# The sample's attention in blocks of 16 rows by 8 columns, with queries and keys put in column order

## The chip, the cores and the metric

The kernel runs on one core of a Trainium2 chip. The metric is the device time of one execution in microseconds; the time shown is the median of three. Five engines run side by side, each through its own list of instructions in a fixed order: PE (matmuls and transposes), DVE (vector), ACT (scalar), POOL (GpSimd) and SP, which here only issues DMAs. They wait for each other through semaphores.

## What is computed

One encoder layer is applied to two sequences, a sample of 1024 tokens and a prompt of 512 tokens, both with 1024 channels. Tokens form a grid of 64 columns, so the sample has 16 rows and the prompt 8. Cut to what matters:

```python
proj = rms_norm(x, norm_g) @ w_in        # u_pool, g_pool, q, k, v, g_attn, 512 columns each
pool_out = pool_mixer(u_pool) * silu(g_pool)
q = rms_norm(q per head) * 64 ** -0.5;  k = rms_norm(k per head)      # 8 heads of 64
# a query in row r, column c sees 8 rows from clip(r - 4, 0, rows - 8)
# and 16 columns from clip(c - 8, 0, 48), with a learned bias by row and column offset
p = softmax(q . k + rpb[h, row offset, column offset])
y = x + concat(pool_out, (p @ v) * silu(g_attn)) @ w_out
```

Products are made in split precision: a value is kept as a rounded high part and a low part (high plus low is the value), and a product is two or three matmuls.

## The kernel before

**Order of the work.** The code records every instruction in a planner (class `Plan`), which gives each a cost and a priority, follows what each tile is read and written by, and then issues all instructions in the order of its own timeline. So all instructions of the profile bear one line, L330, and one has to go by tile names. Where code says `plan.choice()`, the planner also decides the engine. Matmuls of the projections have a lower priority (`MAIN`); PE's list has those of the attention between them where the planner had them ready.

**Stages.** The sample is first. For each of four pairs of heads p: `project_qkv` multiplies the tokens, 128 a tile (t = 0 to 7), into PSUM banks `acc_s_t`; ACT copies them to `qkv_s` (a ring of four); q and k are normalised on DVE, and two transposes per token tile put them into a PSUM bank `ptq_s`, channels by tokens, for two token tiles together (t0 = 0, 2, 4, 6). From there ACT writes the high parts of q and k (`q`, `k`) and DVE the low parts, which sum with the high parts to the values. v goes to DRAM (`vd`) and back into `vs`. Gates (`accg`), the pooling input (`accu`) and the pooling follow. Then the prompt does the same, and at the end both are multiplied by `w_out` (`acco`). The tiles q and k exist once; the next pair overwrites them. In the first pair four token tiles are projected at once.

**Attention.** A block has 128 queries. Before, a block of the sample is 8 rows by 16 columns: for each head, two row tiles (`rt`) of four column blocks (`cb`). It sees 12 rows of keys by 24 (first and last column block) or 32 columns. Each block does: two score matmuls into `s_s`; one DVE operation that adds the bias tile and takes the maximum, into `ns`; the exponential on ACT with its sum; a reciprocal and a rescale; transposes of the probabilities by chunks of 128 keys (`pt_s`); a high and a low part of them (`pp_s`); one value matmul for each chunk (`po_s`, 256 columns: high and low). `ns` is 384 wide, so there are always three chunks, and unseen columns in it stay zero. Every second block the two products are summed (`pv`) and multiplied into the gate (`sg`). Queries are stored with rows and columns reversed inside a block, so that the bias of all queries of a block can be read from one small table (`tab` in DRAM) with a step per query; the bias tile of a head and row tile takes 6 or 7 DMAs.

Of the kernel before, what the change touches and what calls it, by code (L numbers as in the profile page):

```python
# [338 lines left out]
def encoder(ctx, tc, xn_p, xt_p, xn_s, xt_s, w_in, w_out, w_pool, pscale, ng, qg, kg,  # L339
# [63 lines left out]
    def bias_rows(out, h, ro, q0, nq, a):  # L403

        o = tab.offset + (h * 15 + ro) * 32
        if nq == 1:
            sp.dma_start(out=out[16 * q0:16 * q0 + 16, :, a:a + 256],
                         in_=bass.AP(tab.tensor, o, [[HR * 32, 16], [8 * HR * 32, 3], [1, 256]]))
            return
        for ct in range(3):  # L410
            sp.dma_start(out=out[16 * q0:16 * (q0 + nq), ct, a:a + 256],
                         in_=bass.AP(tab.tensor, o + ct * 8 * HR * 32, [[32, nq], [HR * 32, 16], [1, 256]]))

    def load_bias(bt, kind, h):
        if kind == "all":
            bias_rows(bt, h, 0, 0, 8, 0)
        elif kind == "top":
            bias_rows(bt, h, 3, 3, 5, 0)
            for q in range(3):
                bias_rows(bt, h, 3, q, 1, (3 - q) * 32)  # L420
        else:
            bias_rows(bt, h, 0, 0, 4, 128)
            for q in range(4, 8):
                bias_rows(bt, h, 3, q, 1, (7 - q) * 32)
# [63 lines left out]
    ns_edge = {cb: sb.tile([P, 384], F32, name=f"ns_edge_{cb}") for cb in (0, 3)}  # L488
    bias = [sb.tile([P, 3 * 384], F32, name=f"bias_{i}") for i in range(2)]
# [3 lines left out]
    class Sequence:  # L493


        def __init__(self, sq, S, kt_rows, hts, Rb):
# [60 lines left out]
        def project_qkv(self, p, w, group=1):  # L557
# [3 lines left out]
            for t0 in range(0, self.NT, 2):  # L561
# [33 lines left out]
                for i, t in enumerate((t0, t0 + 1)):  # L595
# [7 lines left out]
                    pe.transpose(pt[:, i * P:(i + 1) * P], in_=qkv[:, 0:P], identity=ident)  # L603
                    pe.transpose(pt[:, 256 + i * P:256 + (i + 1) * P], in_=qkv[:, P:256], identity=ident)
# [4 lines left out]
                rt, r0 = (2 * t0) // 8, (2 * t0) % 8  # L609
                lo, hi = 7 - r0, 3 - r0  # L610
                qa = slice(base + rt * 512, base + (rt + 1) * 512)
                ka = slice(base + t0 * P, base + t0 * P + 256)
# [4 lines left out]
                for hd in range(2):
                    for rows in (own[hd], own[1 - hd]):
                        v = q[hd][rows, qa].rearrange("p (cb r c) -> p r cb c", cb=4, r=8)
                        q_dst.append(v[:, lo::-1, :, ::-1] if hi < 0 else v[:, lo:hi:-1, :, ::-1])  # L620
                for hd in range(2):
                    for rows in (own[hd], own[1 - hd]):
                        act.activation(out=k[hd][rows, ka], in_=k_src[hd], func=AF.Copy, scale=gqk[own[hd]])
# [20 lines left out]

        def attention(self, p):
            for hd in range(2):
                for rt in range(self.NB):
                    h = 2 * p + hd
                    kind, i = (("top", 0), ("bot", 1))[rt] if self.S == 1024 else ("all", h % 2)
                    bt = bias[i][:, 0:3 * self.KEYS].rearrange("p (t c) -> p t c", t=3)  # L650
                    load_bias(bt, kind, h)
                    self.head_rows(p, hd, rt, bt)

        def head_rows(self, p, hd, rt, bt):
            sq, KEYS, base = self.sq, self.KEYS, self.base(p)
            h, lo, rbase = 2 * p + hd, hd * HD, 4 * rt

            g = sg[lo:lo + HD, base + rt * 512:base + (rt + 1) * 512]
            for cb in range(4):
                nm = f"{sq}_{h}_{rt}_{cb}"  # L660
                s = bank("s", f"s_{nm}")
                qo = base + rt * 512 + cb * P

                c0, n = CK[cb]

                def kv(x):
                    return x[:, base:base + self.S].rearrange("p (r c) -> p r c", c=GW)[
                        :, rbase:rbase + self.kt_rows, C0[cb] + c0:C0[cb] + c0 + n]

                def seen(x):  # L670
                    return x.rearrange("p (r c) -> p r c", c=32)[:, :, c0:c0 + n]
                sv = s[:, 0:self.kt_rows * n]
                pe.matmul(sv, lhsT=q[hd][:, qo:qo + P], rhs=kv(k[hd]), start=True, stop=False)
                pe.matmul(sv, lhsT=q[hd][:, qo:qo + P], rhs=kv(k[2 + hd]), start=False, stop=True)
                ns = (ns_edge[cb] if cb in ns_edge else ring("ns", 2, [P, 384], f"ns_{nm}"))[:, 0:KEYS]
                nv = seen(ns)
                sm = ring("sm", 3, [P, 3], f"sm_{nm}")
                dve.tensor_tensor_reduce(out=nv, in0=sv.rearrange("p (r c) -> p r c", c=n), in1=seen(bt[:, CT[cb]]), scale=-1.0, scalar=3e38,
                                         op0=ALU.add, op1=ALU.min, accum_out=sm[:, 0:1])
                act.activation(out=nv, in_=nv, func=AF.Exp, scale=-1.0, bias=sm[:, 0:1], accum_out=sm[:, 1:2])  # L680
                dve.reciprocal(out=sm[:, 2:3], in_=sm[:, 1:2])
                with plan.choice():
                    dve.tensor_scalar(out=nv, in0=nv, scalar1=sm[:, 2:3], scalar2=None, op0=ALU.mult)
                    act.activation(out=nv, in_=nv, func=AF.Copy, scale=sm[:, 2:3])
                pt = bank("pt", f"pt_{nm}")
                for c in range(self.CH):
                    pe.transpose(pt[:, c * P:(c + 1) * P], in_=ns[:, c * P:(c + 1) * P], identity=ident)
                pp = ring("pp", 2, [P, 2, 384], f"pp_{nm}", F32R)
                split(pp[:, 0, 0:KEYS], pp[:, 1, 0:KEYS], pt[:, 0:KEYS])

                if cb % 2 == 0:
                    po = bank("po", f"po_{nm}").rearrange("p (cb s q) -> p cb s q", cb=2, s=2)
                for c in range(self.CH):
                    v = vs[base // 256 + rt + c]
                    pe.matmul(po[:, cb % 2], lhsT=v[:, cb, hd * P:(hd + 1) * P], rhs=pp[:, :, c * P:(c + 1) * P],
                              start=c == 0, stop=c == self.CH - 1)
                if cb % 2:
                    pv = ring("pv", 1, [P, 2, P], f"pv_{nm}")[0:HD]
                    act.activation(out=pv, in_=po[HD:P, :, 0], func=AF.Copy)
                    dve.tensor_tensor(out=pv, in0=po[0:HD, :, 1], in1=pv, op=ALU.add)  # L700
                    dve.tensor_tensor(out=pv, in0=po[0:HD, :, 0], in1=pv, op=ALU.add)
                    gv = g.rearrange("p (r cb c) -> p r cb c", r=8, cb=4)[:, :, cb - 1:cb + 1]
                    dve.tensor_tensor(out=gv, in0=pv.rearrange("p cb (r c) -> p r cb c", r=8)[:, ::-1, :, ::-1],
                                      in1=gv, op=ALU.mult)
            sp.dma_start(out=self.mixed[4 + p, lo:lo + HD, rt * 512:(rt + 1) * 512], in_=g)
# [368 lines left out]
```

## Time and profile before

| | |
|---|---|
| median of 3 runs | 649.03 us (647.99 to 649.19) |
| the profiled execution | 648.4 us, span of its instructions 646.6 us |
| granted TensorE clock | 1.00 |
| PE, DVE, ACT, POOL busy | 98%, 86%, 58%, 16% |
| value matmuls `po_s`, transposes `pt_s`, score matmuls `s_s` | 192, 192, 128 |
| loads of v and of the sample's bias | 64 and 104 DMAs |

Busy is the time in which an engine had an instruction under way. Matmuls overlap their predecessors, so the pace of PE is read from the ends of successive rows and not from the mean duration. The sample's attention lies between 60 and 360 us, the prompt's up to about 545 us, and the last 100 us are the output projection.

### The profile page before, as it was taken

How to read it: one execution, taken by the hardware profiler on the slowest of the kernel's cores; microseconds unless marked ns; L12 is line 12 of the kernel's file. 1: busy time of each engine (PE TensorE's matmuls, PEld its weight loads, DVE VectorE, ACT ScalarE, POOL GpSimd, SP SyncE). 2: the span in 40 equal slices, each digit the busy share in tenths (PEclk: the TensorE clock that was granted, in tenths of full speed). 3: DMA queues.
4: the chain of work that ended last, by engine and by line, in shares of the span. 5: the costliest groups of instructions: out<-in, count | busy, mean ns of one | idle time of the engine just before them, and what ended most of it. 6: DMA issues, size and time to landing. Idle time of an engine off the chain costs nothing.

```text
span 646.6 us, 11390 instructions
## 1 busy us (share of the span) xinstructions
PE 635.0 (98%) x3404; PEld 567.0 (88%) x3404; DVE 557.1 (86%) x1647; ACT 372.8 (58%) x910; POOL 100.6 (16%) x142
## 2 busy tenths in 40 slices
PE   6999999999999999999999999999999999999997
PEld 5998899988899888999889989899899878887886
DVE  6688999899987999967999989989999989879742
ACT  5766786568656476544777556477566457323210
POOL 1130100000000000101001110021212423405412
PEclk9999999999999999999999999999999999999999
DMA  8974354442274522425344355545556687843631
GB/s 304 348 205 143 104 169 124 123 121 79 59 246 137 182 62 69 134 95 152 127 112 143 109 168 162 174 139 144 169 174 195 189 261 231 269 152 118 191 131 65
DMA packets 92961, 101.53 MB, mean 157 GB/s; under 512 B 12900, under 2 KB 78564, under 8 KB 92900
## 3 DMA queue, kind: packets, MB, share of 16 engines
q1 hardware_dynamic: 92900, 100.81, 50.7%
q8 instruction: 27, 0.44, 0.3%
q14 instruction: 34, 0.28, 0.1%
HBM read 81.41 MB, written 19.37 MB: 156 GB/s over the span
## 4 chain that ended last, share of the span: by engine, by line
PE 91%; DVE 4%; DMA 3%; issue 1%; ACT 0%; SPq 0%; DVEq 0%; ACTq 0%
PE acc_s L330 21%; PE acco L330 15%; PE accg_s L330 14%; PE acc_p L330 10%; PE accu_s L330 7%; PE accg_p L330 6%; PE po_s L330 4%; PE accu_p L330 3%; PE pt_s L330 3%; PE s_s L330 3%; DMA xr<-in_xn_s 1%; PE po_p L330 1%; PE ptq_s L330 1%; DVE B L330 1%; PE pt_p L330 1%
## 5 line engine op out<-in xcount | busy, mean ns | idle before, releaser
L330 PE MATMUL acc_s<-w_sA,ht_s 128*128 128x384 f32 x768 | 145.9, 342 | 6.3 <-DVE w_sA L330 6.3
L330 PEld LDWEIGHTS acc_s<-w_sA,ht_s 128*128 128x128 f32 x768 | 136.0, 190 | 7.6 <-ACT ht_s L330 5.9
L330 PE MATMUL accg_s<-ht_s,w_sT 128*128 128x512 f32 x384 | 100.4, 399 | 0.0
L330 PEld LDWEIGHTS accg_s<-ht_s,w_sT 128*128 128x128 f32 x384 | 70.0, 188 | 12.0
L330 PE MATMUL acc_p<-w_pA,ht_p 128*128 128x384 f32 x384 | 75.4, 339 | 0.7 <-DVE w_pA L330 0.5
L330 PEld LDWEIGHTS acc_p<-w_pA,ht_p 128*128 128x128 f32 x384 | 66.1, 188 | 1.8 <-DVE w_pA L330 0.8
L330 PE MATMUL acco<-B,left 128*128 128x512 f32 x228 | 56.2, 395 | 0.6 <-DVE left L330 0.6
L330 PE MATMUL accu_s<-ht_s,w_sT 128*128 128x512 f32 x192 | 53.0, 400 | 0.0
L330 PEld LDWEIGHTS acco<-B,left 128*128 128x128 f32 x228 | 41.9, 188 | 9.5 <-DVE left L330 1.0
L330 PE MATMUL accg_p<-ht_p,w_pT 128*128 128x512 f32 x192 | 47.6, 395 | 0.0
L330 PEld LDWEIGHTS accg_p<-ht_p,w_pT 128*128 128x128 f32 x192 | 35.3, 188 | 6.9
L330 ACT ACTIVATE k<-ptq_s,gqk 64x256 fp32r<-64x256 f32 x64 | 30.1, 470 | 18.8 <-PE ptq_s L330 18.1
L330 PEld LDWEIGHTS accu_s<-ht_s,w_sT 128*128 128x128 f32 x192 | 34.6, 188 | 5.1
L330 DVE TENSOR_TENSOR xr<-acco,xr 128x512 f32<-128x512 f32 x30 | 20.5, 686 | 20.4 <-PE acco L330 18.2
L330 ACT ACTIVATE ns_edge<-ns_edge,sm_s 128x288 f32<-128x288 f32 x54 | 28.4, 529 | 16.5 <-DVE sm_s L330 16.3
L330 ACT ACTIVATE ns_s<-ns_s,sm_s 128x384 f32<-128x384 f32 x53 | 31.7, 610 | 10.1 <-DVE sm_s L330 9.9
L330 DVE TENSOR_TENSOR pp_s<-pt_s,pp_s 128x384 fp32r<-128x384 f32 x64 | 34.5, 544 | 0.3
L330 PE MATMUL po_s<-pp_s,v 128*128 128x256 f32 x192 | 32.0, 287 | 0.0
L330 PE MATMUL s_s<-k,q 128*128 128x288 f32 (+1 forms) x128 | 31.4, 330 | 0.0
L330 PEld LDWEIGHTS po_s<-pp_s,v 128*128 128x128 f32 x192 | 28.9, 188 | 1.5
L330 POOL TENSOR_TENSOR vt_s<-qkv_s,vt_s 128x128 fp32r<-128x128 f32 x17 | 9.1, 540 | 122.0 <-ACT vt_s L330 97.3
L330 ACT ACTIVATE qkv_s<-acc_s,rr_s 128x384 f32<-128x384 f32 x24 | 13.7, 578 | 23.6 <-PE acc_s L330 20.9
(221 smaller groups left out, 1350.4 us busy)
## 6 DMA issues: line engine op xcount, KB each, us to landing
v<-vd_s SPq DMA_DIRECT2D x64, 128.0 KB
wr_sA<-in_w_in SPq DMA_DIRECT2D x32, 192.0 KB
wr_sT<-in_w_in SPq DMA_DIRECT2D x32, 192.0 KB
wr_pA<-in_w_in SPq DMA_DIRECT2D x32, 192.0 KB
wr_pT<-in_w_in SPq DMA_DIRECT2D x32, 192.0 KB
out<-xr SPq DMA_DIRECT2D x24, 256.0 KB
x<-in_xt_s SPq DMA_DIRECT2D x16, 256.0 KB
vd_s<-vt_s SPq DMA_DIRECT2D x32, 128.0 KB
```

What stands on the lines that cost most here:

```text
L330: op.fn()
```

## The change

Only the sample's attention changes. Its blocks become 16 rows by 8 columns: for each head eight column blocks. All rows are among the keys; a block sees 23 columns (16 x 23 = 368 keys, `KS`) or, at both ends, 16 (256 keys, `EDGE`). The keys and queries are laid out column by column (column major, 16 rows each), so a block's keys are one contiguous stretch. A block at an end has two chunks instead of three.

The order by columns comes from the transposes of q and k: their second operand is no longer the identity `ident` but `by_column`, two copies of it with its columns permuted (for q reversed too), made once on POOL. ACT and DVE then write each pair of token tiles into runs of two rows in each of 64 columns. The low part of a key pair is written in two instructions instead of one. v is loaded back in column order, eight DMAs a pair, once all token tiles of the pair are stored, and into two sets of buffers in turn. The bias needs a second table (`tab_s`, masked where a row offset is out of the window), built from a transposed copy of the bias (`rel_ts`) by POOL copies and DMAs; the bias of a head is one tile, loaded in 3 DMAs. The fills of the bias tiles with the mask value go; the four `ns` tiles are filled with zeros, two of them again ahead of the prompt. The prompt's attention computes as before. Cut to the core:

```diff
+    by_column = [sb.tile([P, P], F32, name=f"by_column_{x}") for x in "qk"]
+    tab_s = [dram.tile([8, 16, 32, 16], F32, name=f"tab_{i}") for i in range(2)]
...
     def build_table():
+        pe.transpose(rt_ps[0:32, 0:HR], in_=rel[0:HR, 48:80], identity=ident[0:HR, 0:HR])
+        act.activation(out=rt[0:32, 0:HR], in_=rt_ps[0:32, 0:HR], func=AF.Copy)
+        for a in (0, 7):
+            sp.dma_start(out=tab_s[1][:, :, 23 * a // 7:23 * a // 7 + 7], in_=n)
+        for h in range(0, 8, 2):
+            t = staged(f"tab_s_{h}")
+            pool.memset(t[0:32], NEG)
+            for dst, step, src, move, n in ((56, 15, 3, 0, 9), (192, 16, 4, 1, 4), (8, 16, 0, 1, 3)):
+                pool.tensor_copy(out=at(t, dst, [256, 2], [step, n]), in_=at(rt, 15 * h + src, [15, 2], [move, n]))
+            tv = t.rearrange("p (q c) -> p q c", c=16)
+            sp.dma_start(out=tab_s[0][h:h + 2].rearrange("h q d c -> d (h q) c"), in_=tv[0:32])
+            sp.dma_start(out=tab_s[1][h:h + 2, :, 7:23].rearrange("h q d c -> d (h q) c"), in_=tv[7:23])
...
+    def load_bias(bt, sample, h):
+        if sample:
+            for i, first, a, n in ((0, 8, 0, EDGE), (1, 0, EDGE, KS), (0, 0, EDGE + KS, EDGE)):
+                sp.dma_start(out=bt[:, a:a + n],
+                             in_=bass.AP(t.tensor, t.offset + (h * 512 + first) * 16, [[16, 8], [512, 16], [1, n]]))
+            return
...
-                    pe.transpose(pt[:, i * P:(i + 1) * P], in_=qkv[:, 0:P], identity=ident)
-                    pe.transpose(pt[:, 256 + i * P:256 + (i + 1) * P], in_=qkv[:, P:256], identity=ident)
+                    for x, at in enumerate((i * P, 256 + i * P)):
+                        pe.transpose(pt[:, at:at + P], in_=qkv[:, x * P:(x + 1) * P],
+                                     identity=ident if self.S == 512 else by_column[x])
...
+                    def rows_of(x, r):
+                        return x.rearrange("p (c r) -> p c r", r=16)[:, :, r:r + 4].rearrange(
+                            "p c (i r) -> p i c r", r=2)
...
-                    low(k[2 + hd][own[hd], ka], k_src[hd], k[hd][own[hd], ka], gqk[own[hd]])
+                    out, src, high = k_block(k[2 + hd][own[hd]]), k_src[hd], k_block(k[hd][own[hd]])
+                    for i in range(2 if self.S == 1024 else 1):
+                        low(*[x[:, i] if self.S == 1024 else x for x in (out, src, high)], gqk[own[hd]])
...
+                if self.S == 1024:
+                    if t0 == 6:
+                        for j in range(8):
+                            sa = bass.AP(vd.tensor, vd.offset + 8 * j * 256, [[256, 8], [GW * 256, 16], [1, 256]])
+                            sp.dma_start(out=vs[p % 2 * 2 + j // 4][:, j % 4].bitcast(F32), in_=sa)
+                    continue
...
+        def sample_block(self, p, hd, cb, bt, g):
+            first, a, n = ((0, 0, EDGE) if cb == 0 else (6, EDGE + KS, EDGE) if cb == 7 else (cb - 1, EDGE, KS))
+            ks = slice(first * P, first * P + n)
+            gv = g.rearrange("p (r cb c) -> p cb c r", r=16, cb=8)[:, cb - 1:cb + 1] if cb % 2 else None
+            self.block(p, hd, cb, q[hd][:, cb * P:(cb + 1) * P], k[hd][:, ks], k[2 + hd][:, ks], bt[:, a:a + n],
+                       ns[cb % 4], lambda x: x[:, 0:n],
+                       [vs[p % 2 * 2 + j // 4][:, j % 4] for j in range(first, first + (n + P - 1) // P)],
+                       gv, lambda x: x.rearrange("p cb (c r) -> p cb c r", c=8))
```

The planner lays all instructions out anew. Three places show it.

PE, pair 0, the first block of the attention (score matmuls `s_s`; `ptq_s_6` is the transpose of the last two token tiles; `accu` and `accg` are projections). Before:

```order
L330 MATMUL accu_s_1_302<-ht_s_1_117,w_sT_3_160 128x512 x3
L330 MATMUL ptq_s_6_203<-ident,more_85 128x128 x4
L330 MATMUL s_s_0_0_213<-k_94,q_92 128x288
L330 MATMUL s_s_0_1_218<-k_94,q_92 128x384
L330 MATMUL accu_s_1_302<-ht_s_1_118,w_sT_4_162 128x512 x3
L330 MATMUL accu_s_1_302<-ht_s_1_119,w_sT_5_164 128x512 x3
L330 MATMUL s_s_0_0_213<-k_96,q_92 128x288
L330 MATMUL s_s_0_1_218<-k_96,q_92 128x384
```

And in the changed kernel:

```order
L332 MATMUL accg_s_1_256_306<-ht_s_1_119,w_sT_0_158 128x512 x3
L332 MATMUL accg_s_1_256_306<-ht_s_1_120,w_sT_1_160 128x512 x3
L332 MATMUL accg_s_1_256_306<-ht_s_1_121,w_sT_2_162 128x512 x2
L332 MATMUL s_s_0_223<-k_97,q_95 128x256
L332 MATMUL s_s_1_228<-k_97,q_95 128x368
L332 MATMUL accg_s_1_256_306<-ht_s_1_121,w_sT_2_162 128x512
L332 MATMUL accg_s_1_256_306<-ht_s_1_122,w_sT_3_164 128x512
L332 MATMUL s_s_0_223<-k_99,q_95 128x256
```

The first scores have moved behind 44 more projection matmuls: the second half of `accu_s_1`, all of `accg_s_0_256` and a third of `accg_s_1_256`.

PE, the end of pair 0's attention, where the projection of pair 1 (`acc_s_4` to `acc_s_7`, three banks) meets the transposes of its q and k (`ptq_s_0`, `ptq_s_2`). Before:

```order
L330 MATMUL acc_s_4_349<-w_sA_5_322,ht_s_1_119 128x384 x2
L330 MATMUL ptq_s_0_335<-ident,qkv_s_0_330 128x128 x2
L330 MATMUL acc_s_4_349<-w_sA_5_322,ht_s_1_119 128x384
L330 MATMUL ptq_s_0_335<-ident,qkv_s_1_333 128x128 x2
L330 MATMUL acc_s_4_349<-w_sA_6_324,ht_s_1_120 128x384 x3
L330 MATMUL acc_s_4_349<-w_sA_7_326,ht_s_1_121 128x384 x3
L330 MATMUL acc_s_5_352<-w_sA_0_312,ht_s_1_114 128x384 x3
```

And in the changed kernel:

```order
L332 MATMUL acc_s_5_354<-w_sA_7_328,ht_s_1_126 128x384 x3
L332 MATMUL ptq_s_0_337<-by_column_q,qkv_s_0_332 128x128
L332 MATMUL ptq_s_0_337<-by_column_k,qkv_s_0_332 128x128
L332 MATMUL ptq_s_0_337<-by_column_q,qkv_s_1_335 128x128
L332 MATMUL ptq_s_0_337<-by_column_k,qkv_s_1_335 128x128
L332 MATMUL acc_s_6_361<-w_sA_0_314,ht_s_1_119 128x384 x3
L332 MATMUL ptq_s_2_347<-by_column_q,qkv_s_2_342 128x128
L332 MATMUL ptq_s_2_347<-by_column_k,qkv_s_2_342 128x128
L332 MATMUL ptq_s_2_347<-by_column_q,qkv_s_3_345 128x128
L332 MATMUL ptq_s_2_347<-by_column_k,qkv_s_3_345 128x128
L332 MATMUL acc_s_7_362<-w_sA_0_314,ht_s_1_119 128x384 x3
```

The transposes have moved from the middle of `acc_s_4` to the end of `acc_s_5`, and three matmuls of `acc_s_6` and four transposes are what is left between them and `acc_s_7`.

DVE, pair 0, the low parts of q and k of the first two token tiles (`k_96`, `k_97` before and `k_99`, `k_100` after are the low tiles of the two heads; `st_s` are the factors of the normalisation). Before:

```order
L330 TENSOR_TENSOR st_s_4_190<-st_s_4_190 128x8
L330 SCALAR_TENSOR_TENSOR k_96<-ptq_s_0_179,gqk,k_94 64x256
L330 TENSOR_TENSOR q_92<-ptq_s_0_179,q_92 64x4x4x16
L330 SCALAR_TENSOR_TENSOR k_97<-ptq_s_0_179,gqk,k_95 64x256
L330 TENSOR_TENSOR q_93<-ptq_s_0_179,q_93 64x4x4x16
```

And in the changed kernel:

```order
L332 SCALAR_TENSOR_TENSOR k_99<-ptq_s_0_183,qk_t,k_97 64x64x2
L332 TENSOR_TENSOR q_95<-ptq_s_0_183,q_95 64x2x64x2
L332 SCALAR_TENSOR_TENSOR k_99<-ptq_s_0_183,qk_t,k_97 64x64x2
L332 SCALAR_TENSOR_TENSOR k_100<-ptq_s_0_183,qk_t,k_98 64x64x2
L332 TENSOR_TENSOR q_96<-ptq_s_0_183,q_96 64x2x64x2
L332 SCALAR_TENSOR_TENSOR k_100<-ptq_s_0_183,qk_t,k_98 64x64x2
```

Each low part of a key is now two instructions of half the size, and the innermost run of the q and k writes is 2 elements instead of 16 or all.

More of the change, by code (lines that the diff above doesn't have):

```diff
@@ L36 @@
 CT = (2, 1, 1, 0)
+KS = 16 * 23
+EDGE = 256
 BANKS = dict(acc=3, s=2, pt=2, po=1)
@@ L401, in build_table @@
             sp.dma_start(out=tab[16 * half:16 * half + 16].rearrange("q h c -> h q c"), in_=t)
[L403 to L408, printed above, removed]
+    def load_bias(bt, sample, h):
+        if sample:
+            for i, first, a, n in ((0, 8, 0, EDGE), (1, 0, EDGE, KS), (0, 0, EDGE + KS, EDGE)):
+                t = tab_s[i]
+                sp.dma_start(out=bt[:, a:a + n],
+                             in_=bass.AP(t.tensor, t.offset + (h * 512 + first) * 16, [[16, 8], [512, 16], [1, n]]))
             return
         for ct in range(3):
[L411 to L424, printed above, removed]
+            sp.dma_start(out=bt[:, ct * EDGE:ct * EDGE + EDGE],
+                         in_=bass.AP(tab.tensor, tab.offset + (ct * 8 * HR + h * 15) * 32,
+                                     [[32, 8], [HR * 32, 16], [1, EDGE]]))
     def split(out_h, out_l, src, scale=None):
@@ L486, in encoder @@
     vs = [ring("v", 4, [P, 4, 256], f"v_{i}", F32R) for i in range(4)]
-    ns_edge = {cb: sb.tile([P, 384], F32, name=f"ns_edge_{cb}") for cb in (0, 3)}
-    bias = [sb.tile([P, 3 * 384], F32, name=f"bias_{i}") for i in range(2)]
+    ns = [sb.tile([P, 384], F32, name=f"ns_{i}") for i in range(4)]
+    bias = [sb.tile([P, D], F32, name=f"bias_{i}") for i in range(2)]
     hts_s = [[halves(f"ht_s_{c}_{b}") for c in range(KC)] for b in range(2)]
@@ L617, in project_qkv @@
+                q_dst = [q_block(q[hd][rows]) for hd in range(2) for rows in (own[hd], own[1 - hd])]
                 for hd in range(2):
                     for rows in (own[hd], own[1 - hd]):
[L619 to L623, printed above, removed]
+                        act.activation(out=k_block(k[hd][rows]), in_=k_src[hd], func=AF.Copy, scale=gqk[own[hd]])
@@ L646, in attention @@
             for hd in range(2):
[L647 to L705, printed above, removed]
@@ new lines, in attention @@
+                h = 2 * p + hd
+                bt = bias[h % 2]
+                load_bias(bt, self.S == 1024, h)
+                g = sg[hd * HD:hd * HD + HD, self.base(p):self.base(p) + self.S]
+                for cb in range(self.S // P):
+                    if self.S == 1024:
+                        self.sample_block(p, hd, cb, bt, g)
+                    else:
+                        self.prompt_block(p, hd, cb, bt, g)
+                sp.dma_start(out=self.mixed[4 + p, hd * HD:hd * HD + HD], in_=g)
@@ new lines, in prompt_block, with kv, seen @@
+        def prompt_block(self, p, hd, cb, bt, g):
+            base, (c0, n) = self.base(p), CK[cb]
+            def kv(x):
+                return x[:, base:base + 512].rearrange("p (r c) -> p r c", c=GW)[:, :, C0[cb] + c0:C0[cb] + c0 + n]
+            def seen(x):
+                return x[:, 0:EDGE].rearrange("p (r c) -> p r c", c=32)[:, :, c0:c0 + n]
+            qo = base + cb * P
+            gv = g.rearrange("p (r cb c) -> p r cb c", r=8, cb=4)[:, :, cb - 1:cb + 1] if cb % 2 else None
+            self.block(p, hd, cb, q[hd][:, qo:qo + P], kv(k[hd]), kv(k[2 + hd]), seen(bt[:, CT[cb] * EDGE:]),
+                       ns[cb], seen, [vs[base // 256 + c][:, cb] for c in range(2)],
+                       gv, lambda x: x.rearrange("p cb (r c) -> p r cb c", r=8))
@@ new lines, in block @@
+        def block(self, p, hd, cb, qh, kh, kl, bv, ns, seen, v, gv, fold):
+            h, chunks = 2 * p + hd, len(v)
+            nm = f"{self.sq}_{h}_{cb}"
+            s = bank("s", f"s_{nm}")
+            dims = bv.shape[1:]
+            sv = s[:, 0:dims[0]] if len(dims) == 1 else s[:, 0:dims[0] * dims[1]]
+            pe.matmul(sv, lhsT=qh, rhs=kh, start=True, stop=False)
+            pe.matmul(sv, lhsT=qh, rhs=kl, start=False, stop=True)
+            if len(dims) == 2:
+                sv = sv.rearrange("p (r c) -> p r c", c=dims[1])
+            nv = seen(ns)
+            sm = ring("sm", 3, [P, 3], f"sm_{nm}")
+            dve.tensor_tensor_reduce(out=nv, in0=sv, in1=bv, scale=-1.0, scalar=3e38, op0=ALU.add, op1=ALU.min,
+                                     accum_out=sm[:, 0:1])
+            act.activation(out=nv, in_=nv, func=AF.Exp, scale=-1.0, bias=sm[:, 0:1], accum_out=sm[:, 1:2])
+            dve.reciprocal(out=sm[:, 2:3], in_=sm[:, 1:2])
+            with plan.choice():
+                dve.tensor_scalar(out=nv, in0=nv, scalar1=sm[:, 2:3], scalar2=None, op0=ALU.mult)
+                act.activation(out=nv, in_=nv, func=AF.Copy, scale=sm[:, 2:3])
+            pt = bank("pt", f"pt_{nm}")
+            for c in range(chunks):
+                pe.transpose(pt[:, c * P:(c + 1) * P], in_=ns[:, c * P:(c + 1) * P], identity=ident)
+            pp = ring("pp", 2, [P, 2, 384], f"pp_{nm}", F32R)
+            split(pp[:, 0, 0:chunks * P], pp[:, 1, 0:chunks * P], pt[:, 0:chunks * P])
+            if cb % 2 == 0:
+                self.po = bank("po", f"po_{nm}").rearrange("p (cb s q) -> p cb s q", cb=2, s=2)
+            po = self.po
+            for c in range(chunks):
+                pe.matmul(po[:, cb % 2], lhsT=v[c][:, hd * P:(hd + 1) * P], rhs=pp[:, :, c * P:(c + 1) * P],
+                          start=c == 0, stop=c == chunks - 1)
+            if cb % 2:
+                pv = ring("pv", 1, [P, 2, P], f"pv_{nm}")[0:HD]
+                act.activation(out=pv, in_=po[HD:P, :, 0], func=AF.Copy)
+                dve.tensor_tensor(out=pv, in0=po[0:HD, :, 1], in1=pv, op=ALU.add)
+                dve.tensor_tensor(out=pv, in0=po[0:HD, :, 0], in1=pv, op=ALU.add)
+                pv = fold(pv)
+                pv = pv[:, :, ::-1, ::-1] if self.S == 1024 else pv[:, ::-1, :, ::-1]
+                dve.tensor_tensor(out=gv, in0=pv, in1=gv, op=ALU.mult)
@@ L779, in encoder @@
         pool.memset(k[2 + hd][HD - hd * HD:P - hd * HD].bitcast(F32), 0.0)
-    for t in ns_edge.values():
+    for t in ns:
         pool.memset(t, 0.0)
-    for bt in bias:
-        pool.memset(bt, NEG)
     for p in range(NPAIR):
@@ L819, in encoder @@
     pool.memset(U[:, 520:536], 0.0)
+    for cb in (0, 3):
+        pool.memset(ns[cb], 0.0)
     pool.memset(U[:, 1048:1056], 0.0)
```

49 lines of the change are left out of this document (33 added, 16 removed).

## The prediction

> **What bounds the kernel now.** I read the busy totals of the page first, then the stages, then who TensorE waits for, and last the chain. The first two lines are the span and the busy times of the profiled execution.
>
> ```profile
> span 646.6 us, 11390 instructions
> PE 635.0 (98%) x3404; PEld 567.0 (88%) x3404; DVE 557.1 (86%) x1647; ACT 372.8 (58%) x910; POOL 100.6 (16%) x142
> ```
>
> The stages, each with length, then busy time and count of PE, weight load, DVE, ACT and POOL, then granted clock and DMA:
>
> ```profile
> 0.00:20.00 20.00, 13.70 (x64) 13.33 (x65) 14.49 (x29) 12.29 (x18) 2.94 (x9) 1.00 0.91 321
> 60.00:360.00 300.00, 300.00 (x1713) 274.59 (x1712) 271.14 (x840) 194.71 (x475) 18.57 (x30) 1.00 0.42 124
> 80.00:160.00 80.00, 80.00 (x480) 74.74 (x479) 75.84 (x250) 55.67 (x139) 3.60 (x7) 1.00 0.43 127
> 300.00:350.00 50.00, 50.00 (x271) 43.41 (x270) 48.00 (x146) 34.53 (x82) 2.88 (x4) 1.00 0.47 137
> 360.00:600.00 240.00, 238.44 (x1231) 207.43 (x1230) 218.93 (x626) 134.12 (x348) 58.48 (x77) 1.00 0.58 177
> 600.00:646.60 46.60, 42.87 (x188) 34.83 (x186) 22.45 (x37) 5.59 (x12) 12.81 (x10) 1.00 0.39 130
> ```
>
> The sample's attention lies between 60 and 360 us. PE has no gap there, at full clock. DVE has 28.9 us free of the 300, but only 4.2 us in 80 to 160 and 2.0 us in 300 to 350. All that PE waits for another engine:
>
> ```profile
> PE acc_s L330 <- DVE w_sA L330: 6.3, 2, 5.9
> PE acco L330 <- DVE left L330: 0.6, 1, 0.6
> PE acc_p L330 <- DVE w_pA L330: 0.5, 1, 0.5
> PE acc_p L330 <- ACT w_pA L330: 0.2, 1, 0.2
> ```
>
> The 6.3 us are the start, the rest is 1.3 us. Since a busy PE could still run below its rate, I look at the pace in the chain of work that ended last (shares, then start, length, what, count):
>
> ```profile
> PE 91%; DVE 4%; DMA 3%; issue 1%; ACT 0%; SPq 0%; DVEq 0%; ACTq 0%
> ...
> 119.56 10.83 PE acc_s L330 x62
> ...
> 302.46 5.50 PE accg_s L330 x24
> ```
>
> A 384-column matmul takes 10.83 / 62 = 0.175 us and a 512-column one 5.50 / 24 = 0.229 us, so 0.054 us per 128 columns (0.42 ns a column). PE is the bound; a matmul less is worth its pace, as long as DVE, next in line, keeps up.
>
> **PE's part of the change.** For the pace of the attention's matmuls I take ends (start plus length) of successive rows of PE in a piece of attention:
>
> ```profile
> 92.83 1.21 PE L330 MATMUL acc_s<-w_sA,ht_s 128*128 128x384 f32 x6
> 93.88 0.30 PE L330 MATMUL s_s<-k,q 128*128 128x288 f32 x1
> 94.01 0.49 PE L330 MATMUL pt_s<-ident,ns_s 128*128 128x128 f32 x3
> 94.26 0.38 PE L330 MATMUL s_s<-k,q 128*128 128x288 f32 x1
> 94.47 0.34 PE L330 MATMUL acc_s<-w_sA,ht_s 128*128 128x384 f32 x1
> 94.65 0.52 PE L330 MATMUL s_s<-k,q 128*128 128x384 f32 x2
> 95.00 1.03 PE L330 MATMUL acc_s<-w_sA,ht_s 128*128 128x384 f32 x5
> 95.88 0.51 PE L330 MATMUL po_s<-pp_s,v 128*128 128x256 f32 x3
> ```
>
> The ends are 94.04, 94.18, 94.50, 94.64, 94.81, 95.17, 96.03 and 96.39: a score matmul costs 0.14 (288 columns) and 0.18 us (384), a transpose (94.50 - 94.18) / 3 = 0.11 us, a value matmul (96.39 - 96.03) / 3 = 0.12 us.
> - Chunks: per head 8 blocks of 3 chunks become 6 of 3 and 2 of 2, so 24 transposes and 24 value matmuls become 22. For 8 heads: 16 x 0.11 + 16 x 0.12 = 3.7 us less.
> - Scores: per head 4 x 288 + 4 x 384 = 2688 key columns become 6 x 368 + 2 x 256 = 2720. Two matmuls each, 8 heads: 512 columns x 0.42 ns = 0.2 us more.
> - One transpose more for the table: 0.1 us. The transposes of queries and keys stay 64 in number; only their second operand is another tile.
>
> PE's net: -3.7 + 0.2 + 0.1 = -3.4 us, in the stretch where PE never waits.
>
> **DVE's part.** It is off the path now; what matters is whether it stays so. Its groups (busy us, mean ns, idle before):
>
> ```profile
> L330 DVE TENSOR_TENSOR pp_s<-pt_s,pp_s 128x384 fp32r<-128x384 f32 x64 | 34.5, 544 | 0.3
> L330 DVE SCALAR_TENSOR_TENSOR k<-ptq_s,gqk,k 64x256 fp32r<-64x256 f32 x32 | 15.4, 483 | 8.1 <-ACT q L330 7.6
> L330 DVE TENSOR_TENSOR q<-ptq_s,q 64x256 fp32r<-64x256 f32 x32 | 13.5, 422 | 0.6
> L330 DVE TENSOR_TENSOR sg<-pv_s,sg 64x256 f32<-64x256 f32 x32 | 13.6, 425 | 0.5
> L330 DVE TENSOR_TENSOR pv_s<-po_s,pv_s 64x256 f32<-64x256 f32 x64 | 26.0, 407 | 0.2 <-ACT pv_s L330 0.2
> L330 DVE TENSOR_TENSOR pp_p<-pt_p,pp_p 128x256 fp32r<-128x256 f32 x32 | 12.9, 411 | 0.4 <-ACT pp_p L330 0.4
> L330 DVE CAST pp_s<-pt_s 128x384 fp32r<-128x384 f32 x19 | 10.2, 548 | 0.0
> L330 DVE TENSOR_SCALAR ns_s<-ns_s,sm_s 128x384 f32<-128x384 f32 x11 | 4.9, 446 | 0.1
> L330 DVE TENSOR_SCALAR ns_edge<-ns_edge,sm_s 128x288 f32<-128x288 f32 x10 | 3.6, 363 | 0.1
> L330 DVE TENSOR_TENSOR S<-bias,S 128x256 fp32r<-128x256 f32 x11 | 7.3, 675 | 0.4 <-ACT S L330 0.4
> ```
>
> From 384 to 256 columns a low part goes from 544 to 411 ns, 133 ns for 128 columns.
> - The low part of a sample's key pair becomes two instructions of 64x128: 483 - 133 = 350 ns each, 64 x 0.350 - 15.4 = +7.0 us. They stand in DVE's queue behind ACT's q and k copies, and the attention's score matmuls wait for them.
> - 16 low parts and 8 high parts of the probabilities shrink to 256 columns: 24 x 133 ns = -3.2 us. (By the order DVE has 19 high parts in both.)
> - The rescale by the reciprocal goes from 21 to 26 instructions on DVE by the order, at 0.35 to 0.45 us: +2 us. The score-plus-bias operations have 32 columns a head more: 256 x 133 / 128 ns = +0.3 us.
> - New access patterns, which no row prices. Queries and keys are written in runs of 2 elements 16 apart (before: runs of 16, or contiguous), and the gate product (sg, 32 instructions) reads and writes elements 64 apart. The nearest row below is q at 422 ns beside the contiguous pv_s at 407 ns: runs of 16 cost 15 ns. The nearest above is S at 675 ns for 256 columns, the slowest such group. So 0 to 0.25 us each: 0 to 8 us for sg, and 0 to 16 us for the 32 q and 64 key halves together (half length: 0.13 us each). I take 0 to 0.1 us for sg and nothing for runs of two, since q is nearest.
>
> So far +6 to +9 us on DVE, +30 at the upper ends. The first fits into 28.9 us free, the last doesn't.
>
> [...] The sum would move only by what DVE then passes on to PE, which is the second rival.
>
> **ACT, POOL, DMA.** ACT is 58% busy and issues 21 instructions fewer. POOL gets 25 more, all off PE's path but for one: the second broadcast of the row factors now stands behind two fills and six table copies.
>
> ```profile
> 45.04 0.79 POOL L330 COPY ze<-rr_s 128x512 f32<-128x512 f32 x1 [5.32 <-DVE st_s L330]
> ```
>
> A table copy of before took 280 to 534 ns (median 360):
>
> ```profile
> L330 POOL COPY tab<-rel x4: 280/360/534, 27.5 to 28.6; 120x288 f32<-120x288 f32 x1, 120x112 f32<-120x112 f32 x1, 120x256 f32<-120x256 f32 x1, 120x128 f32<-120x128 f32 x1
> ```
>
> Six are 2.2 us, and POOL was idle for 5.3 us before that broadcast: covered, else up to 1 us on PE at its transposes. The SP queue issues 110 DMAs fewer (value loads 64 to 32, the sample's bias loads 104 to 24, stores of the heads 16 to 8; 10 more for the table). The table DMAs of the first two heads and the two fills with the mask value come before the first bias load, which the first score-plus-bias operation waits for. Bias loads and those operations of before (ns min/median/max, first and last start):
>
> ```profile
> L330 SPq DMA_DIRECT2D bias<-tab x128: 303/538/872, 42.1 to 493.7; - x128
> L330 DVE CUSTOM_DVE_ANT_1 ns_edge<-s_s,bias x32: 426/440/459, 66.7 to 355.0; 128x288 f32<-128x288 f32 x32
> ```
>
> They were issued from 42.1 us and first used at 66.7 us, and the first block now stands later still in PE's row, so over 20 us hide them. The values are loaded after the last two token tiles instead of group by group; 8 issues for a pair, and the scores, softmax and transposes of the first block come in between.
>
> **Waits added.** Keys and queries in column order mean that every token tile writes into all columns. So the next pair's first copies must wait for the last block of the head before, and the transposes' bank with them; the copies queue on ACT ahead of evictions. At the first pair's end PE now has only 3 + 4 small instructions (0.53 + 0.44 us) between the transposes of q and k and acc_s_7, which needs the eviction of acc_s_4 (578 ns on ACT) with two semaphore hops.
>
> ```profile
> L330 ACT ACTIVATE qkv_s<-acc_s,rr_s 128x384 f32<-128x384 f32 x24 | 13.7, 578 | 23.6 <-PE acc_s L330 20.9 <-issue 2.4
> ```
>
> I put 0.7 us there and at like places (bounds: 0, as PE waits for nothing there now, and the 3 us of the last rival).
>
> **Sum.** -3.4 + 0.7 = -2.7 us. The profiled execution took 648.4 us (its span 646.6 and 1.8 around it), 0.6 us less than the median of 649.03: it becomes 645.7 us, the median 646.3 us.
>
> **Rivals.**
> 1. DVE eats the gain. It is 95 to 96% busy in the dense stretches, and PE is in order. With +9 to +15 us a pair's share is 2 to 4 us against 4.2 us free in 80 to 160; PE then waits about 1 us at each of three pair ends, 3 us in all: 649 us, no change. For it: the lack of free time. Against: PE now waits nowhere with DVE at 96%, and the order gives DVE's work that can go elsewhere to ACT and POOL.
> 2. DVE becomes the bound (slower). With sg at the upper end and part of the scattered writes DVE gets +22 us, 5.5 a pair. The 4.2 us free around a pair's end can be used by half, as inputs come late, so DVE is 1.3 (all used) to 3.4 us behind when PE stands at the transposes without other matmuls. Three pair ends: 4 to 10 us, 649.6 to 655.8, middle 652.6 us. From 1.6 us per pair end (4.7 us over three) it decides for slower.
> 3. The saving comes whole and the new order also loses the 1.3 us of small waits: 649.0 - 3.4 - 1.3 = 644.3 us.
>
> **How the numbers follow.** A measurement can tell about 0.2% (1.3 us) from no change. The forecast (644.9 to 647.7 us, most of it near 646.3) gets 0.49; the third rival 0.07, the first 0.21, the second 0.23. The forecast and the third rival are faster (0.56), the first is the same but for 0.01 (0.20), and that and the second are slower (0.24). The range for 8 in 10 runs from the third rival's 644.3 to the second's middle, 652.6 us; the forecast's own is 644.9 to 647.7.
>
> **What the profile after would show.** Right: 176 value matmuls and transposes each, PE busy near 632 us, 60 to 360 still without a gap, sg near 430 ns and the key halves near 350. Wrong: PE waits on DVE or ACT at the pair ends (acc_s, ptq_s), sg above 600 ns, DVE above 570 us, or transposes that take longer with the permuted operand.

## The result and the profile after

The changed kernel takes 653.0 us (median of 4 runs, 651.91 to 653.94) against 648.51 for the kernel before, run beside it: ratio 1.0069, 95% interval 1.0056 to 1.0082, about 4.5 us slower. The forecast was 646.3 us and faster. The profiled execution took 653.36 us. First its span and busy times:

```profile
span 651.6 us, 11209 instructions
PE 636.2 (98%) x3373; PEld 562.5 (86%) x3373; DVE 570.8 (88%) x1697; ACT 363.2 (56%) x889; POOL 107.8 (17%) x167
```

The same stages as before (length, then busy time and count of PE, weight load, DVE, ACT and POOL, clock, DMA):

```profile
60.00:360.00 300.00, 297.82 (x1677) 269.48 (x1675) 279.82 (x882) 191.99 (x468) 25.13 (x39) 1.00 0.34 101
80.00:160.00 80.00, 79.69 (x471) 72.97 (x470) 77.62 (x262) 55.04 (x138) 4.82 (x9) 1.00 0.29 84
300.00:350.00 50.00, 48.65 (x254) 41.40 (x253) 47.23 (x137) 31.78 (x74) 4.02 (x4) 1.00 0.39 116
360.00:600.00 240.00, 236.31 (x1218) 204.13 (x1217) 219.14 (x631) 129.51 (x340) 53.91 (x73) 1.00 0.58 177
```

PE now has gaps in the sample's attention (2.2 us of 300), and DVE is 8.7 us busier there. What PE waits for (left out: the start of 5.9 us, and two waits of 0.4 and 0.5 us at the output projection), and the chain that ended last, which ran through DVE for 4% before:

```profile
PE s_p L332 <- DVE q L332: 1.4, 1, 1.4
PE po_s L332 <- DVE pp_s L332: 1.3, 1, 1.3
PE accm_p L332 <- DVE ph L332: 0.9, 1, 0.9
PE po_s L332 <- DVE pv_s L332: 0.8, 2, 0.5
PE po_s L332 <- DVE st_s L332: 0.2, 1, 0.2
...
PE 76%; DVE 15%; DMA 4%; ACT 2%; issue 2%; SPq 0%; ACTq 0%
```

The value matmuls of the sample (`po_s`) wait for DVE, which they never did; the other new waits (`s_p`, `accm_p`) lie at 523 to 536 us, where the prompt ends. The groups that the change touches:

```profile
L332 DVE TENSOR_TENSOR sg<-pv_s,sg 64x256 f32<-64x256 f32 x32 | 22.9, 717 | 0.5
L332 DVE SCALAR_TENSOR_TENSOR k<-ptq_s,qk_t,k 64x128 fp32r<-64x128 f32 x64 | 22.4, 349 | 5.3 <-ACT q L332 3.9 <-ACT k L332 0.2
L332 DVE TENSOR_TENSOR q<-ptq_s,q 64x256 fp32r<-64x256 f32 x32 | 13.5, 423 | 0.5
L332 PE MATMUL po_s<-pp_s,v 128*128 128x256 f32 x176 | 30.2, 287 | 2.4 <-DVE pp_s L332 1.3 <-DVE pv_s L332 0.8 <-DVE st_s L332 0.2
L332 PE MATMUL pt_s<-ident,ns 128*128 128x128 f32 x176 | 29.8, 272 | 0.0
```

The gate product went from 425 to 717 ns (32 of them: +9.3 us of DVE). The other rows of DVE's sum came near what was worked out: key halves +7.0 us, parts of the probabilities -3.2, rescale about +3 for 2. The dearest single place, DVE's rows at 340 us (start, length, what):

```profile
340.00 1.53 DVE L332 TENSOR_TENSOR sg<-pv_s,sg 64x256 f32<-64x256 f32 x1
341.45 0.54 DVE L332 TENSOR_TENSOR w_pA<-wr_pA,w_pA 128x384 fp32r<-128x384 f32 x1
341.91 1.22 DVE L332 CAST w_pA<-wr_pA 128x384 fp32r<-128x384 f32 x1
343.05 0.54 DVE L332 TENSOR_TENSOR pp_s<-pt_s,pp_s 128x384 fp32r<-128x384 f32 x1
```

PE stands from 342.3 to 343.64 us until that `pp_s` is there. POOL had two additions under way meanwhile (339.89 to 342.92); the other 31 products took 0.64 to 0.91 us.

A second thing shows in PE's pace, where it waits for nothing. Rows of the chain, before and then after:

```profile
55.37 5.50 PE accu_s L330 x24
588.08 52.07 PE acco L330 x226
```

```profile
55.13 4.43 PE accu_s L332 x19
142.93 4.66 PE accu_s L332 x20
216.04 6.78 PE accg_s L332 x29
592.50 47.69 PE acco L332 x204
```

A 512-column matmul took 0.229 to 0.230 us before and takes 0.233 to 0.234 now. Summed over the ends of successive matmuls, the 1404 of `accg`, `accu` and `acco` need 3.6 us more (waits left out). No step of the prediction had this.

So two questions: is the gate product the cause of the waits (theory A) or the new order (theory B), and what slowed the pace? The program gives one lead for the second: the small tiles ahead of the large ones have changed (`by_column` is new, `gqk` is no longer a tile of its own), and that shifts addresses. By the program's layout q, k, v and the 16 halves of `ht` began at multiples of 64 bytes in SBUF; now they begin 32 bytes past one (theory C).

### The profile page after: what moved, and what is told of

It reads as the page before. It is cut to its first block, busy times and chain, and to the rows that moved or that the text cites. A ratio compares the mean times of both kernels' runs of the same rounds, so it can differ in the third digit from the quotient of the medians.

```text
span 651.6 us, 11209 instructions
## 1 busy us (share of the span) xinstructions
PE 636.2 (98%) x3373; PEld 562.5 (86%) x3373; DVE 570.8 (88%) x1697; ACT 363.2 (56%) x889; POOL 107.8 (17%) x167
## 4 chain that ended last, share of the span: by engine, by line
PE 76%; DVE 15%; DMA 4%; ACT 2%; issue 2%; SPq 0%; ACTq 0%
PE acc_s L332 18%; PE acco L332 16%; PE accg_s L332 10%; PE acc_p L332 9%; PE accg_p L332 5%; PE accu_s L332 5%; DMA rB<-in_w_out 3%; PE accu_p L332 3%; DVE pp_s L332 2%; PE po_s L332 2%; DVE ns L332 2%; PE s_s L332 2%; PE pt_s L332 2%; DVE pv_s L332 1%; PE s_p L332 1%
## 5 line engine op out<-in xcount | busy, mean ns | idle before, releaser
L332 PE MATMUL acc_s<-w_sA,ht_s 128*128 128x384 f32 x768 | 149.2, 344 | 5.9 <-DVE w_sA L332 5.9
L332 ACT ACTIVATE ns<-ns,sm_s 128x368 f32<-128x368 f32 (+1 forms) x102 | 56.7, 573 | 28.6 <-DVE sm_s L332 28.0
L332 ACT ACTIVATE k<-ptq_s,qk_t 64x256 fp32r<-64x256 f32 x64 | 30.6, 479 | 14.8 <-PE ptq_s L332 14.0
L332 DVE TENSOR_TENSOR pp_s<-pt_s,pp_s 128x384 fp32r<-128x384 f32 (+1 forms) x64 | 32.5, 511 | 0.1
L332 PE MATMUL po_s<-pp_s,v 128*128 128x256 f32 x176 | 30.2, 287 | 2.4 <-DVE pp_s L332 1.3
L332 PEld LDWEIGHTS po_s<-pp_s,v 128*128 128x128 f32 x176 | 26.8, 188 | 5.8 <-issue 2.1
L332 DVE CUSTOM_DVE_ANT_0 ns<-s_s,bias 128x368 f32<-128x368 f32 (+1 forms) x64 | 30.9, 495 | 0.1
L332 PE MATMUL s_s<-k,q 128*128 128x368 f32 (+1 forms) x128 | 30.1, 330 | 0.0
L332 ACT ACTIVATE ns<-ns,sm_p 128x256 f32<-128x256 f32 (+1 forms) x53 | 24.0, 476 | 10.8 <-DVE sm_p L332 10.6
L332 PE MATMUL pt_s<-ident,ns 128*128 128x128 f32 x176 | 29.8, 272 | 0.0
```

The lines of the kernel that those rows point to most:

```text
L332: op.fn()
```

## The experiments

Each ratio is against the kernel before, five rounds on the same chip, with its 95% interval. The experiments ran on three chips; across chips only the ratios are compared.

**The gate product in plain order, two ways.** First, permute where PSUM is read (shortened):

```diff
+ top, hi, lo = [fold(x)[:, ::-1, :, ::-1] for x in (po[HD:P, :, 0], po[0:HD, :, 0], po[0:HD, :, 1])]
- act.activation(out=pv, in_=po[HD:P, :, 0], func=AF.Copy)      # and both additions alike
+ act.activation(out=pv, in_=top, func=AF.Copy)                 # pv: rows, blocks, columns
- gv = g.rearrange("p (r cb c) -> p cb c r", r=16, cb=8)[:, cb - 1:cb + 1]
+ gv = g.rearrange("p (r cb c) -> p r cb c", r=16, cb=8)[:, :, cb - 1:cb + 1]
```

> The changed kernel with the gate product in plain order: the step from rows to columns is taken when the products are read out of PSUM (one ACT copy and two DVE additions for each pair of blocks read PSUM in steps of 16 elements and write SBUF in runs of 16 or longer), and the gate product reads and writes runs of 16. The order of instructions on every engine stays that of the changed kernel. Theory A (the gate product with elements 256 bytes apart makes DVE late, and PE's waits of the middle stages come from it): the product falls from 717 to about 430 ns, 9 us less on DVE, PE's waits between 100 and 400 us (3.6 us) nearly vanish, 648.5 to 650.5 us. Theory B (the new order of the work makes the waits, whatever one product takes): 652 to 653.5 us. If PSUM read in steps is slow too, the additions and ACT's copies rise above 407 ns and the time stays above 651.

Second, only the last line, with the result `pv` read in steps of 16 elements:

> The changed kernel with the same gate product walked in another order: rows outermost and the 16 columns of two blocks innermost, so that the gate is read and written in runs of 16 elements and only the attention's result is read in steps of 16 elements (64 bytes). Same order of instructions on every engine. [...] Theory B: 652 to 653.5 us.

Measured: 648.63 us, ratio 1.0007 (0.9993 to 1.0021), and 650.52 us, 1.0043 (1.0031 to 1.0055). The product in the first, the additions that now read PSUM in steps, the wait that is left; then the product in the second:

```profile
L332 DVE TENSOR_TENSOR sg<-pv_s,sg 64x256 f32<-64x256 f32 x32 | 14.9, 464 | 0.5
L332 DVE TENSOR_TENSOR pv_s<-po_s,pv_s 64x256 f32<-64x256 f32 x64 | 26.1, 408 | 0.7 <-ACT pv_s L332 0.6
PE po_s L332 <- DVE pp_s L332: 0.8, 1, 0.8
```

```profile
L332 DVE TENSOR_TENSOR sg<-pv_s,sg 64x256 f32<-64x256 f32 x32 | 21.0, 656 | 0.5
```

Theory A holds: with the same order on every engine, the plain product brings 1.0069 down to 1.0007, some 4 us. PE's idle time between 100 and 400 us falls from 2.5 to 0.8 us. The sample's value matmuls (duration in ns, then first and last start) show where the time is won, in the changed kernel and in the first variant:

```profile
L332 PE MATMUL po_s<-pp_s,v x176: 274/281/386, 86.6 to 369.7; 128*128 128x256 f32 x176
L332 PE MATMUL po_s<-pp_s,v x176: 274/282/384, 86.5 to 366.5; 128*128 128x256 f32 x176
```

From the first to the last PE needs 280.0 us instead of 283.1, so 3.1 us of the gain lie there. The wait that is left stands at the place that was at 340 us. There the plain product still took 1.28 us, beside POOL's two additions again, and PE waited 0.8 us for the `pp_s` behind it. So the step explains only a part of that one wait; whether POOL explains the rest was not tried.

Steps of 64 bytes in PSUM cost DVE nothing (408 against 407 ns); in SBUF, on one operand of three, they cost 190 ns where 256 bytes on two cost 243 (median of one 612 ns, against 665 in the changed kernel and 422 plain). For the second I had estimated 430 to 600 ns and 648.5 to 651 us: the mean of 656 ns missed the first, 650.52 us fell within the second.

**The slow product in the kernel before.** Same stretch of the gate, walked by columns (`"p (r cb c) -> p cb c r"`). The result is read in the same shape, so the products meet the wrong gates.

> The kernel before with the sample's gate product walked column by column, elements 64 apart (256 bytes), over the same stretch of the gate; the values of the attention's half of the output are not those of the layer, since products meet the wrong gates. The order of all instructions is that of the kernel before. Theory A: the product goes from 425 to about 700 ns, 9 us more on DVE, and PE, which waits nowhere between 60 and 360 us in the kernel before, begins to wait there: 1.5 to 5 us longer, 650 to 653.5 us. Theory B: the kernel before has 28.9 us free on DVE in this stretch and takes the 9 us without loss: under 649.5 us.

Measured: 650.09 us, 1.0038 (1.0024 to 1.0052). The product took 641 ns (about 700 expected), 32 times 216 ns or 7 us more:

```profile
L330 DVE TENSOR_TENSOR sg<-pv_s,sg 64x256 f32<-64x256 f32 x32 | 20.5, 641 | 0.5
60.00:360.00 300.00, 298.75 (x1698) 271.48 (x1698) 274.20 (x836) 193.42 (x472) 17.67 (x30) 1.00 0.41 124
```

PE gets gaps (1.25 us) where it had none: theory A again. DVE's 28.9 us of free time in this stretch did not absorb all of the 7: 2.0 us came through by the medians.

**The planner told of the product's time.** One term in its cost: `+ (290 if far else 0)`.

> The changed kernel with the planner told what the gate product takes (290 ns more); nothing else. The order of all engines is laid out anew. Theory A: the planner puts DVE's work that has a choice on ACT and POOL and the matmuls that depend on late results further back, so part of the 5 us is won back: 650 to 652 us. Theory B: the order changes but is not better: 651.5 to 655 us.

Measured: 662.17 us, 1.0224 (1.021 to 1.0238), a miss of both. One wait makes most of it, for the pooling of the last pair, and the clock is low behind it. The wait, then windows (clock is the last but two):

```profile
PE accm_p L333 <- ACT ph L333: 9.2, 1, 9.2
...
522.00:526.00 4.00, 0.14 (x1) 0.14 (x1) 3.71 (x13) 1.06 (x3) 0.56 (x2) 0.50 0.96 286
526.00:530.00 4.00, 4.00 (x10) 3.14 (x11) 3.37 (x12) 1.47 (x3) 0.00 (x0) 0.50 0.81 260
```

So a new order can cost more than what it was meant to mend. That is large enough for theory B, and needed a test by itself (below).

**Addresses.** The first variant with 32 unused bytes ahead of the large tiles, and 32 ahead of the weight buffers so that these stay where they were modulo 64:

```diff
+    sb.tile([P, 8], F32, name="pad_0")
     x_s = [big([P, 2, 512], f"x_{i}") for i in range(8)]
...
+    sb.tile([P, 8], F32, name="pad_1")
```

> The kernel of the first run (gate product in plain order) with two unused tiles of 32 bytes a partition, one ahead of the large tiles and one ahead of the weight buffers. They shift the addresses: q, k, v and the 16 halves of ht begin at multiples of 64 bytes as in the kernel before (without the first tile they lie 32 bytes past one), the weights at multiples of 64 bytes as in both. Order and instructions unchanged. In the traces of the changed kernel and its variants the 512-column matmuls follow each other at 231 to 233 ns (median) and the 384-column ones at 173 to 174; in the kernel before and its variant at 229 to 231 and at 175. Theory C (where the streamed tile begins sets this pace): back to 229 to 231 and 175 ns, about 3.8 us less over the 1224 long matmuls with 1.6 more over the 384-column ones, 645 to 647.5 us. Against it (the pace has another cause, the order of instructions for one): 648 to 649.5 us with the paces unchanged.

The same two lines in the kernel before, where they move the tiles to 32 past a multiple of 64:

> The kernel before with the same two unused tiles, which move q, k, v and the halves of ht to 32 bytes past a multiple of 64 and leave the weights at a multiple. Order and instructions unchanged. Theory C: 512-column matmuls go from 229 to 231 up to 231 to 233 ns and the 384-column ones from 175 to 174: 1.5 to 3 us slower, 649.5 to 651 us. Against it: 648 to 648.5 us and the paces of the kernel before.

And in the changed kernel with its slow product:

> The changed kernel with the two unused tiles of 32 bytes alone: same order, same instructions, the gate product with its step of 256 bytes. Theory C with the pace independent of DVE's lateness: the 512-column matmuls fall back to 229 to 231 ns and the time by the 3 us that the shift was worth with the plain product, 649.5 to 650.5 us. If PE, faster by 3 us, only waits longer for a late DVE: 651 to 653 us, with PE's waits above the 12.5 us of the changed kernel.

Measured: 646.52 us, 0.9959 (0.9946 to 0.9973); 650.08, 1.0020 (1.0010 to 1.0031); 649.25, 1.0015 (1.0004 to 1.0026). The pace in the first, and in the kernel before when shifted:

```profile
54.95 4.35 PE accu_s L332 x19
141.25 4.59 PE accu_s L332 x20
214.21 6.64 PE accg_s L332 x29
585.08 54.81 PE acco L332 x238
```

```profile
55.45 5.60 PE accu_s L330 x24
589.61 50.41 PE acco L330 x216
```

0.229 to 0.230 us again with the pads, 0.233 in the shifted kernel before: theory C, in both directions and at the same instructions. DVE's busy time is the same with the pads as without (562.5 and 563.0 us with the plain product), so the pace isn't an effect of DVE. The pads are worth 3.1 us with the plain product and 3.5 us with the slow one (649.25 us is 0.25 less than the least that I expected). Not all of this need be pace: PE's wait for the prompt's pooling (`accm_p`, 0.8 and 0.9 us) is gone from both lists with the pads. The kernel before lost 1.3 us by the shift. In the two profiled executions, which differ by 2.1 us in span, the sum of its long matmuls grew by 3.1 us, that of the 384-column ones fell by 0.6. The pads move all those tiles together, so which of them sets the pace (the streamed one or the loaded one) stays open.

**The low part of a key once.** Transposes write PSUM interleaved, so that two token tiles' rows lie side by side and 256 elements are one instruction. In a new order (shortened):

```diff
- pe.transpose(pt[:, at:at + P], ...)
+ pe.transpose(pt[:, x * 256:x * 256 + 256].rearrange("p (c i r) -> p i c r", i=2, r=2)[:, i if x else 1 - i], ...)
- for i in range(2): low(out[:, i], src[:, i], high[:, i], gqk[own[hd]])
+ low(out, src, high, gqk[own[hd]])
```

> The shifted kernel with the low part of a key pair in one instruction again: the transposes of two token tiles write PSUM interleaved (64 columns of 2 rows, 4 elements apart), so that queries and keys are read as one stretch of 256 and written in runs of 4. The planner lays out the order anew. Theory A (what DVE does more than before comes back at PE as waits): 32 instructions and about 7 us less on DVE, 1 to 3 us less than the shifted kernel. Theory B (the order of the last pair of the prompt costs most of what is left: PE waits 3.3 us at 520 to 531 us, against 0.9 us before): what counts is whether the new order has projection matmuls again between the last transposes and the last key and query, which by its order it has; 2 to 3 us less, whatever DVE's time. If transposes that write PSUM in steps run slower, PE's 64 of them show it at over 0.13 us each.

In the old order, with the plain product and then with the slow one:

> As the run before, but in the order of the shifted kernel: the planner still counts two low parts for each key pair, the first issues the whole and the second nothing. So it differs from the shifted kernel by 32 DVE instructions alone (about 7 us of DVE) and the layout in PSUM. Theory A: 1 to 3 us less than the shifted kernel, by PE's waits at 341 us and around the first score matmuls. Theory B: at most 0.5 us less, since PE now waits only 1.3 us in the sample's attention and the waits at 520 to 531 us have nothing to do with the sample's keys.

> The run before with the low part of a key pair in one instruction, in the order of the changed kernel: 7 us less on DVE while the gate product keeps its step of 256 bytes. Theory A (what DVE is late, PE waits): with the product slow the 7 us are worth more than the 1.3 us that they were worth with the plain product, 2 to 4 us less than the changed kernel with the shift alone. Theory D (the place counts, not the sum: the slow product lies in the chain from one value matmul to the next, the key's low parts lie elsewhere): 0.5 to 1.5 us less.

Measured: 644.14 us, 0.9928 (0.9915 to 0.9940); 645.19, 0.9947 (0.9930 to 0.9963); 648.92, 1.0004 (0.9993 to 1.0014). In the same order, 7 us less on DVE brought 0.8 us (0.9959 to 0.9947; 1.3 by the medians) and 0.7 us (1.0015 to 1.0004; 0.3 by the medians), which their intervals don't tell from nothing. So by the ratios 1.2 of the 2.0 us that the first is ahead of the padded variant came only with the new order; both theories had allowed the 2.0. Theory A expected more where the product is slow (2 to 4 us) and that fell; the numbers lie nearer theory D, the place and not the sum. By it, where DVE is late counts, not how much it does: the gate product stands in DVE's queue shortly ahead of a `pp_s`, as at 340 us, and the key's low parts don't. (After 24 of the 32 gate products at most 8 instructions come before the next `pp_s`, after each low part of a key at least 13. That this distance decides is read from the order and not tried.) The transposes that write PSUM interleaved kept their pace, 0.109 us each. The first of the three beats both kernels; its busy times and the sample's attention, in which the list of PE's waits names no value matmul:

```profile
PE 630.7 (98%) x3373; PEld 562.7 (88%) x3373; DVE 552.8 (86%) x1663; ACT 363.6 (57%) x892; POOL 104.5 (16%) x166
60.00:360.00 300.00, 299.93 (x1703) 274.34 (x1702) 267.82 (x849) 194.44 (x478) 26.17 (x43) 1.00 0.34 103
```

**A new order alone.** `TO_PE = 800` to `900`, the planner's assumed delay, in the kernel before and in the best variant.

> The kernel before with one number of the planner changed: it assumes 900 instead of 800 ns from the end of an instruction on another engine to the start of the matmul that waits for it. The instructions are the same, their order is new on all engines. Theory B (an order laid out anew has its own gains and losses of some us, mostly where the prompt ends): 1 to 5 us away from the kernel before, to either side, with PE's waits at other places. Against it: within 1 us.

> The fastest variant so far (plain gate product, shifted tiles, key's low part in one instruction) with the same number of the planner changed to 900 ns. Same instructions, new order. Theory B: 1 to 5 us away from that variant, to either side; where it is faster, PE's wait at 525 us has gone. Against it: within 1 us, 643.5 to 645 us.

Measured: 654.13 us, 1.0082 (1.0068 to 1.0096), and 650.29 us, 1.0020 (1.0005 to 1.0035). By the ratios that is 5.3 us slower than the kernel before and 6.0 us slower than the best variant, both more than the 1 to 5 us expected, with the same matmuls (some work that has a choice of engine went elsewhere). Both lose most of it where the prompt ends: of 520 to 545 us PE is busy 21.39 and 21.70, against 24.72 and 24.10. PE in the second, by windows:

```profile
522.00:526.00 4.00, 2.73 (x14) 2.00 (x14) 4.00 (x17) 3.82 (x13) 0.73 (x1) 1.00 0.82 255
526.00:530.00 4.00, 2.65 (x10) 1.86 (x8) 3.06 (x14) 2.46 (x9) 0.00 (x0) 0.56 1.03 333
```

The order has the prompt's scores and values there with few projection matmuls between them; PE waits for DVE five times between 521 and 529 us (0.24 to 0.85 us each), and then the clock falls to 0.56.

## Why the prediction was wrong

- **PE's net of -3.4 us** nearly held: 176 value matmuls and transposes; by ends, the transposes take 1.8 to 2.0 us less in sum (1.76 forecast), the value matmuls 1.3 with the plain product (1.92 forecast), the scores the same (0.2 more forecast). With the two terms below taken out again (plain product, pads) the kernel is at 0.9959, 646.4 us by the median of 649.03; the sum had said 646.3. That they meet to 0.1 us is in part luck: this variant still waits 1.0 us for a `pp_s` and 0.9 us at the prompt's scores, which the sum did not have.
- **DVE's sum: the term that failed is the gate product.** Taken at 0 to 0.1 us, bounded by 0.25 us, it was 0.29 us on the mean (0.24 by the median of one). "q is nearest" was the wrong choice of row: the q of that row is read and written in runs of 16, the gate one element at a time. The rest held: key halves 349 ns (350 forecast), runs of two free (q 423 against 422 ns; ACT's copies of k 479 against 470). For single elements the forecast had no row, only that estimate from rows with longer runs. The runs showed the size for 256 columns: 0.19 us more for one stream in steps of 64 bytes and 0.24 us for two in steps of 256 bytes (by medians, 612 and 665 ns against 422 plain).
- **"The first fits into 28.9 us free"** failed as a way of reasoning. DVE had the time, but PE takes its instructions in order: it waited 1.3 us when one `pp_s` was late (342.3 us), however much DVE rested elsewhere. The kernel before shows it too: 7 us more on DVE, 2.0 us more in all by the medians (1.0038).
- **The small waits of 0.7 us at pair ends** are not there as meant. Eight transposes at 121 to 123 us, at the first pair's end, took 0.64 us more by ends than the 0.109 us each of all others. With the plain product none of this is left, so the gate product made it and not the eviction of `acc_s_4`. POOL's copies and the table's DMAs stayed covered, as said: PE waits for neither.
- **The second rival** named the mechanism (a slow gate product makes DVE late) and its 652.6 us is near the result, but not for its reason: the waits came at value matmuls and only for 0.64 us at a pair's end, and made about 4 us in all. Two of the signs of being wrong came, sg at 717 ns and DVE at 570.8 us. Without the addresses' share (pads, slow product) the kernel stands at 1.0015 (649.25 us), near the first rival, in which DVE eats the gain; that rival too had the waits at pair ends.
- **No rival had the addresses.** They make the other 3.1 to 3.5 us. With the forecast's -2.7, that is -2.7 + 4.0 + 3.3 = +4.6 us, against 4.5 measured.
- **The new order** was taken to be neutral outside the sample. Where the prompt ends it wasn't (PE busy 24.72 us of 520 to 545 before, 22.27 after, 23.70 with the plain product and the pads), but waits of 0.7 us for weights at 473 us went. On balance it cost little in that last variant; the last two runs show that a new order can cost 5 to 6 us.

## What to carry to other kernels

Price an access pattern by the innermost run of each operand (here 0.19 to 0.24 us more for 256 single elements in SBUF, and 423 against 422 ns for runs of two), and take the step from rows to columns where it is free (here in reads of PSUM, 408 against 407 ns). Free time of an engine says little (here DVE had 28.9 us, and 2.0 of its 7 us more came through); ask which instruction of the critical engine waits for the one that grew, and what stands between them. When a change adds or resizes a tile, compare the addresses of all tiles behind it (here 3.1 to 3.5 us), and when a planner lays the work out anew, keep the old order for one run (here a new order alone cost 5 to 6 us), so that the change and the new order are measured apart.

## What the hardware showed unexpectedly

- 32 bytes in the place of the large tiles change PE's pace by 1.5% (0.229 to 0.233 us for 512 columns), both ways, in two kernels.
- In runs where PE had gaps, the granted clock fell: in a wait of 9.2 us it fell to 0.50 and stayed there for the next 4 us, with PE at work throughout, and where PE was busy 2.7 of every 4 us it fell to 0.56 in the second such window. Behind the 9.2 us a 512-column matmul took 0.43 us (1.28 us for three) instead of 0.23, so that wait was paid twice. At 22.27 us busy of 25 (the changed kernel, 520 to 545) the clock stayed at 1.00.
